# A two-block transformer forward pass: memory's key and value weights used whole, the rope tables issued in two parts, output weights by rows

## The chip, the cores and the metric

The kernel runs on one core of one Trainium2 chip. The metric is the time of the whole program on the device, in microseconds.

## The reference

A first block and then a second block of two layers work on 256 tokens of 1024 channels in fp32. Only the first block (and one line of the second) is touched. Cut to what matters it is:

```python
xn = rmsnorm(h, norm_mix_g)
q, k, v, u, y = split(xn @ w_in)             # 512 columns each
q, k = rope(q, positions), rope(k, positions)
attn = dilated_mixture_attention(q, k, v)    # 8 heads of 64
rec = bidirectional_rglru(conv(u), ...) * gelu(y)
h = h + concat([attn, rec]) @ w_out          # 1024 x 1024
hn, mn = rmsnorm(h, norm_cross_g), rmsnorm(mem, norm_mem_g)
q, k, v = hn @ w_cq, mn @ w_ck, mn @ w_cv    # 1024 x 512 each, 4 heads of 128
h = h + softmax(q k^T / sqrt(128)) v @ w_co  # 512 x 1024
hid = square(relu(rmsnorm(h, norm_mlp_g) @ w_mlp_in))
h = h + hid @ w_mlp_out
```

The second block has four mixers a layer (one of them, `mla`, is latent attention with norms of queries and keys) and a gated MLP.

## The kernel before

Activations lie channel by token, in 8 groups of 128 channels by 256 tokens. All large weights are streamed from HBM by SP in one array, `W`, in blocks of eight 128x128 tiles (512 KB, five buffers `w`). Each block is split in two f32r parts: ACT copies it to `whi` (L357) and DVE subtracts, `wlo` (L358), four buffers each. Activations are split the same way (`xh`, `xl`). A product of the precision wanted is then three f32r matmuls: `mm3` (L382 to L384: high by high, high by low part of the activation, low part of the weight by high). `lin` goes through a projection output chunk by output chunk, pairs of 128 columns sharing a PSUM bank; `lin_k` goes row by row of the weight, with all four chunks open in banks side by side; `lin_t` (L649 to L651) uses the activation as the stationary side and gives token by channel. Such results are used by consumers that are put off (`pend`, `flush`, `tick`) so that other work can go between.

Block 1 runs, in order, through w_in's part u (`lin_k`), q, k, v, y, then w_ck (memory's keys), w_out, w_cq, w_cv (memory's values), w_co, and the MLP. Beside these, generators put other work in between: the recurrence (`rglru`), the 8 heads of attention, memory's norm (`mem_prep`), the 4 heads of cross attention. `drive` and `interleave` step them at the chunks' ends, and a list scheduler writes each engine's queue with priorities (`high_priority`, `urgent`); the queues are fixed when the program is built, and each engine works through its own in order.

The first norm of the block needs a power, which runs on POOL (`rpow`, L401, `n1r`); its result is spread over partitions by two matmuls (L419, `n1p`), copied by ACT (L480, `n1b`), and every consumer of w_in multiplies by it. POOL also computes the angles of the rope tables from the positions (`rope_tables`, tiles `rt`, L845 and L850, with one cast L865), 50 small instructions of 128x64, then clears two large tiles (`gb`, L776). `derived` computes small parameters of the recurrence by a series on DVE (tiles `l`, L814 and L816). ACT takes the sine of the angles (L901, L902, `misc<-rt`), and eight matmuls (`rsp`, L911) spread the tables.

A head of attention has scores on PE (L1115, `sc`), scores plus bias and their maximum on DVE (L687, two instructions), the negated maximum (L693, `nm`), two exponentials on ACT (L699, `p`), the reciprocal of the sum on DVE (L702, `rd`), two scalings of `p` on ACT (L710, `times`), four transposes on PE (L717, `ptp`), a copy on ACT (L720, `pts`) and the values on PE (L727, `po`). Cross attention is the same with L1197 for scores and L1207 for values; its scores start at fixed points of w_cv. ACT and DVE then split the heads' output (`mxh`, `mxl`, or `ch`, `cl`), the moving side of w_out and w_co. In w_out the attention half of the rows comes first, and `rec` (the recurrence's output times the gate) is computed before w_out starts.

Of the kernel before, what the change touches and what calls it, by code (L numbers as in the profile page):

```python
# [15 lines left out]
OP = mybir.AluOpType  # L16
# [9 lines left out]
LAYERS = 2  # L26
BRANCHES = (1, 0, 2, 3)
NL, NX = 3, 4
# [5 lines left out]
X0, X1 = 1, 3  # L34
# [32 lines left out]
def plan():  # L67
# [4 lines left out]
    def f(key, idx, cols):  # L72
        p.append((key, idx, cols, "F"))

    def t(key, idx, cols):
        p.append((key, idx, cols, "T"))
# [11 lines left out]
    f("w_out", (0,), r(1024))  # L88
    tf("w_cq", (0,), r(512))
    t("w_cv", (0,), r(512))  # L90
    f("w_co", (0,), r(1024))
# [22 lines left out]
def stream_array(inp):  # L114
    tiles = []
    for key, idx, cols, kind in plan():
        w = np.asarray(inp[key])[idx][:, cols]
        k, n = w.shape
        w = w.reshape(k // 128, 128, n)
        if kind == "F":  # L120
# [154 lines left out]
class Kern:  # L275
    def __init__(self, ctx, tc, a, pcols, ccols, depth=5, ahead=2):
# [25 lines left out]
        for key, idx, cols, kind in plan():  # L302
            self.plan.append((key, idx, len(cols), kind))
        self.seg = 0
# [57 lines left out]
    def wtile(self, n=1):  # L362
# [7 lines left out]
        if o + n == size:  # L370
            self.blk_split.pop(self.pi)
            self.pi += 1
        return hi[:, o * 128:(o + n) * 128], lo[:, o * 128:(o + n) * 128]
# [22 lines left out]
    def rpow(self, name, src, n, mul, add):  # L396
# [4 lines left out]
        self.nc.gpsimd.tensor_tensor(r, v, self.mhalf[:, :n], op=OP.pow)  # L401
# [111 lines left out]
class Body(Kern):  # L513
# [42 lines left out]
    def lin(self, key, idx, M, act, consume, K=KD, fine=False, half=False, m0=0, side=False):  # L556


        for m in range(0, M, 2):
# [3 lines left out]
            for i, (c, k) in enumerate(self.order(key, idx, M, K, m, side)):  # L563
# [10 lines left out]
                if c == n - 1 or one or half:  # L574
# [47 lines left out]
    def lin_k(self, key, idx, M, act, consume, K=KD):  # L622

        self.segment(key, idx, M * 128, "T")
        ps = [self.ps("plk").rearrange("p (c t) -> p c t", c=2) for _ in range(M // 2)]
# [13 lines left out]
    def lin_t(self, key, idx, ncols, act, consume, K=KD, steps=2):  # L639
# [37 lines left out]
    def softmax(self, ps, scale, bias=None, normalize=True):  # L677
# [25 lines left out]
        if normalize:  # L703
            self.times(p, rd)
# [81 lines left out]
    def derived(self):  # L786
# [13 lines left out]
        nc.gpsimd.tensor_tensor(u, one, nab, op=OP.pow)  # L800

# [16 lines left out]
        nc.vector.tensor_tensor(lp, acc, z, op=OP.mult)  # L818
# [13 lines left out]
    def rope_tables(self):  # L832
# [45 lines left out]
        w = tt(turns(k2, P2), turns(k1, P1), OP.add)  # L878
        w = tt(w, rnd(w, 1.0), OP.subtract)
# [68 lines left out]
    def block1(self):  # L948
# [8 lines left out]
        self.derived()  # L957
        self.rope_tables()
# [3 lines left out]
        mh = [self.g4(f"mh{i}", F32R) for i in range(2)]  # L962
        ml = [self.g4(f"ml{i}", F32R) for i in range(2)]
        rm = {}

        def mem_prep():
            nm = Norm(self, eng=V)
            for j in range(4):
# [21 lines left out]
        self.setup_late()  # L990
# [151 lines left out]
        mact = lambda k: (mh[k // 4][:, k % 4], ml[k // 4][:, k % 4])  # L1142
# [4 lines left out]
        def c_cv(half, ps):  # L1147
# [15 lines left out]
        def residual(norm, g, scale=None, also=None):  # L1163
            def f(k, ps, n):
# [8 lines left out]
                if also:  # L1173
# [4 lines left out]
        run(self.lin("w_out", (0,), 8, lambda k: (mix_h[k // 4][:, k % 4], mix_l[k // 4][:, k % 4]),  # L1178
                     residual(n2, self.G("norm_cross_g")), fine=True))
# [657 lines left out]
```

## Time and profile before

| | us |
|---|---|
| runs | 1291.26, 1288.01, 1279.97 (median 1288.01) |
| profiled execution | 1285.87 |
| its span, first to last instruction | 1284.1 |
| PE busy in the span | 1253.4 |
| DVE, ACT, POOL busy | 917.8, 721.5, 85.3 |

Times of the trace count from the start of the span; 1.8 us of the execution lie around it. An idle time in front of an instruction is what its engine waited, and the name behind it is what came last. The granted clock (PEclk) is a share of TensorE's full 2.4 GHz: 1.00 is that level, 0.50 the 1.2 GHz one.

### The profile page before, as it was taken

The numbers are of one execution on the slowest core, as the hardware profiler recorded it, in microseconds if no ns is written. First come the engines' busy times: TensorE is split into PE (matmuls) and PEld (weight loads), VectorE is DVE, ScalarE is ACT, GpSimd is POOL, SyncE is SP. The second block draws the span as 40 slices with busy tenths as digits, with TensorE's granted clock in tenths as the row PEclk, the third lists the DMA queues.
The fourth block names the chain that finished last, engine by engine and source line by source line (L and its number), as shares of the span: only waits on it lengthen the run. The fifth ranks groups of instructions, "written<-read, shape, count | busy, mean of one in ns | idle before, by whom it ended". The sixth has DMA issues, their size and how long they took to land.

```text
span 1284.1 us, 21656 instructions
## 1 busy us (share of the span) xinstructions
PE 1253.4 (98%) x8514; PEld 1143.5 (89%) x8514; DVE 917.8 (71%) x1396; ACT 721.5 (56%) x1132; POOL 85.3 (7%) x105
## 2 busy tenths in 40 slices
PE   8998989999999999999999999999999999999998
PEld 7885978888899998899988888899988999888887
DVE  5996748875577985767777776669867677777754
ACT  5787556554456456644556554464565545655542
POOL 8010000000001201000000000012001000000000
PEclk9899999999999999999999999999998999999999
DMA  7742535555564551345555566544522355555662
GB/s 258 214 140 75 177 97 194 193 188 190 192 231 160 180 172 60 116 154 184 180 188 189 188 216 209 190 153 161 170 99 96 128 187 172 190 191 187 194 191 75
DMA packets 68742, 216.08 MB, mean 168 GB/s; under 512 B 10392, under 2 KB 16280, under 8 KB 68640
## 3 DMA queue, kind: packets, MB, share of 16 engines
q1 hardware_dynamic: 68592, 214.66, 50.9%
q8 instruction: 67, 1.10, 0.4%
q14 instruction: 35, 0.29, 0.1%
q0 software_dynamic: 48, 0.03, 0.0%
HBM read 208.37 MB, written 1.05 MB: 163 GB/s over the span
## 4 chain that ended last, share of the span: by engine, by line
PE 85%; ACT 2%; DVE 1%; DMA 1%; SPq 1%; issue 1%; DVEq 0%; ACTq 0%
PE pw L601 27%; PE pw L602 14%; PE pl L383 11%; PE pl L382 10%; PE pl L384 10%; PE ph L1428 2%; PE pl L649 1%; PE pl L650 1%; PE pl L651 1%; PE pq L1577 1%; SPq L1495 1%; DMA tabs<-in_C_dram 1%; PE pod L727 1%; ACT p L699 1%; PE ptp L717 1%; PE mst L426 1%
## 5 line engine op out<-in xcount | busy, mean ns | idle before, releaser
L357 ACT ACTIVATE whi<-w 128x1024 fp32r<-128x1024 f32 (+1 forms) x386 | 404.2, 1050 | 456.3 <-issue 166.8
L358 DVE TENSOR_TENSOR wlo<-w,whi 128x1024 fp32r<-128x1024 f32 (+1 forms) x386 | 467.2, 1212 | 244.6 <-ACT whi L357 244.0
L601 PE MATMUL pw<-xx,whi 128*128 128x512 f32 x960 | 334.0, 393 | 0.0
L602 PE MATMUL pw<-xx,wlo 128*128 128x256 f32 x960 | 268.2, 280 | 0.0
L382 PE MATMUL pl<-xx,whi 128*128 128x256 f32 x912 | 261.3, 287 | 3.6 <-ACT whi L357 3.6
L384 PE MATMUL pl<-xx,wlo 128*128 128x256 f32 x912 | 261.9, 288 | 1.8 <-DVE wlo L358 1.8
L383 PE MATMUL pl<-xx,whi 128*128 128x256 f32 x912 | 261.2, 287 | 0.0
L601 PEld LDWEIGHTS pw<-xx,whi 128*128 128x128 f32 x960 | 179.6, 187 | 39.9
L382 PEld LDWEIGHTS pl<-xx,whi 128*128 128x128 f32 x912 | 175.7, 193 | 8.2 <-ACT whi L357 4.0
L602 PEld LDWEIGHTS pw<-xx,wlo 128*128 128x128 f32 x960 | 181.1, 189 | 0.2
L384 PEld LDWEIGHTS pl<-xx,wlo 128*128 128x128 f32 x912 | 175.8, 193 | 3.2 <-DVE wlo L358 2.1
L383 PEld LDWEIGHTS pl<-xx,whi 128*128 128x128 f32 x912 | 175.9, 193 | 1.0 <-issue 0.8
L601 PE MATMUL pw<-fw,whi 128*128 128x512 f32 x352 | 123.4, 395 | 1.2 <-DVE fw L391 1.2
L602 PE MATMUL pw<-fw,wlo 128*128 128x256 f32 x352 | 98.9, 281 | 0.8 <-DVE wlo L358 0.8
L601 PE MATMUL pw<-hd,whi 128*128 128x512 f32 x256 | 88.8, 394 | 0.0
L601 PEld LDWEIGHTS pw<-fw,whi 128*128 128x128 f32 x352 | 66.0, 187 | 16.7 <-DVE fw L391 1.5
L602 PE MATMUL pw<-hd,wlo 128*128 128x256 f32 x256 | 70.9, 277 | 0.0
L602 PEld LDWEIGHTS pw<-fw,wlo 128*128 128x128 f32 x352 | 66.5, 189 | 1.4 <-DVE wlo L358 1.4
L601 PEld LDWEIGHTS pw<-hd,whi 128*128 128x128 f32 x256 | 48.0, 188 | 11.2
L602 PEld LDWEIGHTS pw<-hd,wlo 128*128 128x128 f32 x256 | 48.0, 188 | 0.0
L383 PE MATMUL pl<-ol,whi 128*128 128x256 f32 x128 | 37.1, 291 | 0.4 <-DVE ol L391 0.4
L382 PE MATMUL pl<-oh,whi 128*128 128x256 f32 x128 | 37.4, 295 | 0.0
(427 smaller groups left out, 1979.2 us busy)
## 6 DMA issues: line engine op xcount, KB each, us to landing
w<-in_W_dram SPq DMA_DIRECT2D x378, 512.0 KB, 3.5
w<-in_W_dram SPq DMA_DIRECT2D x8, 256.0 KB, 4.6
sw<-in_S_dram SPq DMA_DIRECT2D x4, 512.0 KB, 5.7
h<-in_xT_dram SPq DMA_DIRECT2D x8, 128.0 KB, 4.8
mem<-in_memT_dram SPq DMA_DIRECT2D x2, 512.0 KB, 7.7
sw<-qe SPq DMA_DIRECT2D x16, 64.0 KB, 4.6
dt<-in_C_dram SPq DMA_DIRECT2D x4, 256.0 KB, 8.1
dqs<-dhi SPq DMA_DIRECT2D x16, 64.0 KB, 3.6
```

The source lines that it names most:

```text
L357: self.nc.scalar.activation(hi, w, AF.Copy)
L358: self.nc.vector.tensor_tensor(lo, w, hi.bitcast(F32), op=OP.subtract)
L382: mm(out, wh, xh, start=first, stop=False, skip_group_check=shared)
L383: mm(out, wh, xl, start=False, stop=False, skip_group_check=shared)
L384: mm(out, wl, xh, start=False, stop=last, skip_group_check=shared)
L426: self.nc.tensor.matmul(ps[:, h], s[:, h * 128:h * 128 + 128], e, start=(i == 0), stop=(i == len(squares) - 1))
L601: mm(po[c], wh, x, start=k == 0, stop=False, skip_group_check=True)
L602: mm(po[c][:, 0], wl, x[:, 0], start=False, stop=k == K - 1, skip_group_check=True)
L649: mm(o, xh[:, s], wh, start=(k == 0), stop=False)
L650: mm(o, xh[:, s], wl, start=False, stop=False)
L651: mm(o, xl[:, s], wh, start=False, stop=(k == K - 1))
L1428: nc.tensor.matmul(ps[:, k], hk[:, 2 * hp + k // 2, s], qz[:, 2 * hp + k // 2, s], start=True, stop=True)
```

## The change

`WHOLE`: the blocks of w_ck and w_cv are not split, and neither is memory. Their products are one plain fp32 matmul in the place of three f32r ones (`wl is None`). The streamed block itself is then the operand, so its buffer is held until PE has used it, and the prefetch is limited by that (`kept`).

The rope tables and `derived` become generators in two parts. The first part of each is issued before the first norm's power, the second after it (`issue_after`), with the clearing of `gb`. The series of `derived` is written with seven fused instructions.

The first 512 columns of w_out and w_co go by `lin_k` (four chunks side by side), the other 512 by `lin`. The rows of w_out come in `OUT_ORDER`, the recurrence's half first, and `rec` runs before attention has to be done. The scaling of `p` moves from ACT to DVE (all softmaxes but those of one mixer, which calls `times` itself). Cross attention is driven as an urgent generator over w_cq and w_cv, with its value step later (`X1`). Norms 1 and 2 are spread one step earlier. In `mla` the power of the keys and queries `mrn` is computed before the other, `mqs`.

```diff
+WHOLE = ("w_ck", "w_cv")
+OUT_ORDER = (4, 5, 6, 7, 0, 1, 2, 3)
-X0, X1 = 1, 3
+X0, X1 = 1, 5
...
-    f("w_out", (0,), r(1024))
+    t("w_out", (0,), r(512), OUT_ORDER)
+    f("w_out", (0,), 512 + r(512), OUT_ORDER)
...
-        while self.nd < min(b + self.depth, self.nblk):
+        while self.nd < min([b + self.depth, self.nblk] + [k + NW for k in self.kept[:1]]):
             self._dma()
...
+        if self.ns in self.whole:
+            self.kept.append(b)
+            self.blk_split[self.ns] = (w, None)
+            self.ns += 1
+            return
...
+        if wl is None:
+            mm(out, wh, xh, start=first, stop=last, skip_group_check=shared)
+            return
...
         if normalize:
-            self.times(p, rd)
+            for q in range(2):
+                nc.vector.tensor_scalar(p[:, q], p[:, q], rd[:, q:q + 1], None, op0=OP.mult)
...
-        nc.vector.memset(acc, 1.0 / 17.0)
-        for k in (15, 13, 11, 9, 7, 5, 3, 1):
+        nc.vector.tensor_scalar(acc, z2, 1.0 / 17.0, None, op0=OP.mult)
+        for k in (15, 13, 11, 9, 7, 5, 3):
             nx = self.small("l9", 8)
-            nc.vector.tensor_tensor(nx, acc, z2, op=OP.mult)
-            acc = self.small("l10", 8)
-            nc.vector.tensor_scalar(acc, nx, 1.0 / k, None, op0=OP.add)
+            nc.vector.scalar_tensor_tensor(nx, acc, 1.0 / k, z2, op0=OP.add, op1=OP.mult)
+            acc = nx
...
         w = tt(turns(k2, P2), turns(k1, P1), OP.add)
+        yield
         w = tt(w, rnd(w, 1.0), OP.subtract)
...
-        self.derived()
-        self.rope_tables()
+        small = self.derived()
+        next(small)
+        tables = self.rope_tables()
+        next(tables)
...
-        self.setup_late()
+        self.tick()
+        self.tick()
+        with self.tc.issue_after(self.last_pow.ins):
+            run(tables)
+            self.setup_late()
+        run(small)
...
-        mact = lambda k: (mh[k // 4][:, k % 4], ml[k // 4][:, k % 4])
+        mact = lambda k: (self.mem[k // 4][:, k % 4], None)
...
-                    self.lin("w_ck", (0,), 4, mact, c_ck, half=True), ("need", rg), ("need", at)])
+                    self.lin("w_ck", (0,), 4, mact, c_ck, half=True), ("need", rg), ("need", rec()), ("need", at)])
         self.flush()
-        run(rec())
...
-        run(self.lin("w_out", (0,), 8, lambda k: (mix_h[k // 4][:, k % 4], mix_l[k // 4][:, k % 4]),
-                     residual(n2, self.G("norm_cross_g")), fine=True))
+        run(self.lin_k("w_out", (0,), 4, xmix, res, bank=self.psl))
+        run(self.lin("w_out", (0,), 4, xmix, res, fine=True, m0=4))
...
-        interleave(self.lin_t("w_cv", (0,), 512, mact, c_cv, steps=4), [cross()])
+        at = urgent(self.tc, cross(), HA)
+        self.drive([("begin", at), self.lin("w_cq", (0,), 4, xact, c_cq, half=True, side=True),
+                    self.lin_t("w_cv", (0,), 512, mact, c_cv, steps=4), ("need", at)])
...
+            rn = self.rpow("mrn", st2[:, 8:16], 8, 1.0 / 96, EPS)
             qs = self.small("mqs", 8)
             nc.gpsimd.tensor_tensor(qs, v, self.mhalf[:, :8], op=OP.pow)
-            rn = self.rpow("mrn", st2[:, 8:16], 8, 1.0 / 96, EPS)
```

How the queues move shows at three places. In POOL's queue at the first norm's power (`n1r`; `rt` are the angles), before:

```order
L850 TENSOR_TENSOR rt_243<-rt_243,rt_242 128x64
L845 TENSOR_SCALAR rt_243<-rt_243 128x64 x4
L850 TENSOR_TENSOR rt_243<-rt_243 128x64 x2
L845 TENSOR_SCALAR rt_243<-rt_243 128x64 x2
L776 MEMSET gb_462 128x1024
L776 MEMSET gb_463 128x1024
L401 TENSOR_TENSOR n1r<-v,misc 128x2
L401 TENSOR_TENSOR mr<-v,misc 128x2
```

The same place after:

```order
L874 TENSOR_SCALAR rt_191<-rt_191 128x64
L879 TENSOR_TENSOR rt_191<-rt_190,rt_191 128x64
L874 TENSOR_SCALAR rt_191<-rt_191 128x64
L879 TENSOR_TENSOR rt_191<-rt_191 128x64 x4
L426 TENSOR_TENSOR n1r<-v,misc 128x2
L874 TENSOR_SCALAR rt_191<-rt_191 128x64
L874 TENSOR_SCALAR rt_191<-rt_190 128x64
L924 MEMSET misc 128x1
```

The power stood behind all 50 instructions of the tables and two clearings; now it stands behind 28 of them, and the rest follows it.

In ACT's queue at the sines (`misc<-rt`) and the copy of the spread norm (`n1b`), before:

```order
L357 ACTIVATE whi<-w 128x1024 x3
L902 ACT_TABLE_LOAD
L902 ACTIVATE misc<-rt_243 128x64
L901 ACTIVATE misc<-rt_244,misc 128x64
L357 ACTIVATE whi<-w 128x1024 x4
L480 ACTIVATE n1b<-n1p 128x256
L357 ACTIVATE whi<-w 128x1024
L1013 ACTIVATE uc<-ut,pt 128x256 x4
```

And after:

```order
L377 ACTIVATE whi<-w 128x1024 x3
L505 ACTIVATE n1b<-n1p 128x256
L377 ACTIVATE whi<-w 128x1024 x3
L932 ACT_TABLE_LOAD
L932 ACTIVATE misc<-rt_192 128x64
L377 ACTIVATE whi<-w 128x1024
L931 ACTIVATE misc<-rt_193,misc 128x64
L1049 ACTIVATE uc<-ut,pt 128x256 x4
```

The sines stood in front of four splits and the norm's copy; they now stand behind the copy and behind three of those splits. On PE the two `n1p` matmuls follow the norm's sums (`ss`) by 26 products in the place of some 78, and `rsp` follows `n1p` by some 78 in the place of 60.

In PE's queue where w_ck ends and attention's last heads remain, before (`ptp` transposes, `sc` scores, `po` values):

```order
L384 MATMUL pl<-mh_297,wlo 128x256
L717 MATMUL ptp<-ct,p 128x128
L1115 MATMUL sc<-kr,qr 128x256 x2
L717 MATMUL ptp<-ct,p 128x128 x3
L1115 MATMUL sc<-kr,qr 128x256 x2
L717 MATMUL ptp<-ct,p 128x128 x4
L727 MATMUL po<-pts,vv 64x256 x4
L717 MATMUL ptp<-ct,p 128x128
L1115 MATMUL sc<-kr,qr 128x256 x2
L717 MATMUL ptp<-ct,p 128x128 x3
L1115 MATMUL sc<-kr,qr 128x256 x2
L717 MATMUL ptp<-ct,p 128x128 x4
```

And after, from the last product of w_ck on:

```order
L405 MATMUL pl<-mem_500,w 128x256
L746 MATMUL ptp<-ct,p 128x128 x4
L756 MATMUL po<-pts,vv 64x256
L746 MATMUL ptp<-ct,p 128x128 x4
L756 MATMUL po<-pts,vv 64x256 x3
L1151 MATMUL sc<-kr,qr 128x256 x4
L756 MATMUL po<-pts,vv 64x256
L746 MATMUL ptp<-ct,p 128x128 x8
L756 MATMUL po<-pts,vv 64x256 x3
L746 MATMUL ptp<-ct,p 128x128 x4
L756 MATMUL po<-pts,vv 64x256 x5
L746 MATMUL ptp<-ct,p 128x128 x4
```

Four heads' scores stood behind w_ck; now two do, since two more heads' scores stand among w_ck's products. Behind these rows w_out begins in both; now 24 of its products (`plk`) stand in front of the last three value matmuls, where 13 stood among the last heads before.

## Rows read from the trace of the kernel before

**Rows 1.** The page: span, and busy time of the engines.
```profile
span 1284.1 us, 21656 instructions
...
PE 1253.4 (98%) x8514; PEld 1143.5 (89%) x8514; DVE 917.8 (71%) x1396; ACT 721.5 (56%) x1132; POOL 85.3 (7%) x105
```

**Rows 2.** Busy time by stretch, block 1.
```profile
core 0: us, PE busy (x) PEld busy (x) DVE busy (x) ACT busy (x) POOL busy (x), PEclk, DMA share, GB/s
28.90:32.34 3.44, 0.00 (x1) 0.01 (x1) 1.61 (x2) 1.61 (x4) 3.11 (x8) 0.95 0.00 0
32.34:42.22 9.88, 7.41 (x31) 6.82 (x32) 8.08 (x20) 4.21 (x6) 1.87 (x2) 0.50 0.74 217
42.22:101.10 58.88, 58.67 (x406) 54.08 (x406) 57.84 (x93) 49.97 (x82) 3.88 (x1) 1.00 0.58 178
101.10:126.00 24.90, 18.57 (x98) 11.05 (x97) 16.35 (x48) 20.44 (x53) 0.00 (x0) 0.93 0.15 46
171.70:186.00 14.30, 10.84 (x63) 8.49 (x61) 5.16 (x14) 9.65 (x26) 0.00 (x0) 1.00 0.26 89
```

**Rows 3.** Waits, 0 to 50 us: us in total, times, longest.
```profile
PE pl L382 <- ACT whi L357: 3.6, 2, 3.4
```

**Rows 4.** Timeline of POOL, 7 to 36 us: start, us, instruction [idle before].
```profile
18.20 1.91 POOL L850 TENSOR_TENSOR rt<-rt 128x64 f32<-128x64 f32 x2
20.19 1.17 POOL L845 TENSOR_SCALAR rt<-rt 128x64 f32<-128x64 f32 x1
...
25.20 1.17 POOL L850 TENSOR_TENSOR rt<-rt 128x64 f32<-128x64 f32 x4
...
35.25 1.73 POOL L401 TENSOR_TENSOR n1r<-v,misc 128x2 f32<-128x2 f32 x1 [2.78 <-DVE misc L822]
```

**Rows 5.** Timeline of DVE, same stretch.
```profile
20.05 1.21 DVE L358 TENSOR_TENSOR wlo<-w,whi 128x1024 fp32r<-128x1024 f32 x1
...
30.73 0.23 DVE L891 TENSOR_TENSOR rt<-rt 128x64 f32<-128x64 f32 x1 [7.81 <-POOL rt L845]
```

**Rows 6.** Timeline of PE, 19.5 to 38 us.
```profile
19.90 0.50 PE L426 MATMUL ss<-ct,sq 128*128 128x1 f32 x4
...
37.04 0.69 PE L419 MATMUL n1p<-ct,n1r 128*128 128x128 f32 x2 [0.67 <-POOL n1r L401]
```

**Rows 7.** Timeline of PE, 60 to 68 us: fp32 and f32r products.
```profile
63.57 1.03 PE L1030 MATMUL pga<-uc,gb 128*128 128x256 f32 x4
64.44 1.03 PE L1031 MATMUL pgx<-uc,gb 128*128 128x256 f32 x4
...
67.16 0.39 PE L651 MATMUL pl<-whi,xx 128*128 128x512 f32 x1
...
67.84 0.39 PE L651 MATMUL pl<-whi,xx 128*128 128x512 f32 x1
```

**Rows 8.** Timeline of PE, 99.5 to 126 us: w_ck's end, attention's tail.
```profile
100.62 0.28 PE L384 MATMUL pl<-mh,wlo 128*128 128x256 f32 x1
...
100.98 0.28 PE L384 MATMUL pl<-mh,wlo 128*128 128x256 f32 x1
...
125.22 0.39 PE L383 MATMUL pl<-mxl,whi 128*128 128x256 f32 x1 [0.34 <-DVE mxl L391]
```

**Rows 9.** Instructions by line and shape, ACT, 76 to 124 us: busy, mean ns | idle.
```profile
L710 ACT ACTIVATE p<-p,rd 128x256 f32<-128x256 f32 x16 | 7.2, 499 | 1.5 <-DVE rd L702 1.5
```

**Rows 10.** The same view of DVE, whole span.
```profile
L1553 DVE TENSOR_SCALAR cqa<-cqa,pt 128x256 f32<-128x256 f32 x6 | 1.7, 347 | 0.0
```

**Rows 11.** Timeline of DVE, 99 to 118 us: heads 3 and 7.
```profile
104.74 0.40 DVE L687 CUSTOM_DVE_ANT_0 sb<-sc,lnc 128x256 f32<-128x256 f32 x1
...
115.30 0.42 DVE L687 CUSTOM_DVE_ANT_0 sb<-sc,lnc 128x256 f32<-128x256 f32 x1
```

**Rows 12.** Timeline of PE, 171 to 187 us: cross attention.
```profile
174.36 0.33 PE L717 MATMUL ptp<-ct,p 128*128 128x128 f32 x1 [1.35 <-ACT p L710]
```

**Rows 13.** Timeline of PE, layer 0's mla, 508 to 519 us.
```profile
516.45 0.60 PE L419 MATMUL rnb<-ct,rep 128*128 128x128 f32 x3 [1.00 <-DVE rep L416]
```

More of the change, by code (lines that the diff above doesn't have):

```diff
@@ L70, in plan, with f, t @@
     r = np.arange
[L72 to L76, printed above, removed]
+    def f(key, idx, cols, order=()):
+        p.append((key, idx, cols, "F", order))
+    def t(key, idx, cols, order=()):
+        p.append((key, idx, cols, "T", order))
     def tf(key, idx, cols):
@@ L115, in stream_array @@
     tiles = []
-    for key, idx, cols, kind in plan():
+    for key, idx, cols, kind, order in plan():
         w = np.asarray(inp[key])[idx][:, cols]
@@ L119, in stream_array @@
         w = w.reshape(k // 128, 128, n)
+        if order:
+            w = w[list(order)]
         if kind == "F":
@@ L301, in __init__ @@
         self.plan = []
-        for key, idx, cols, kind in plan():
+        for key, idx, cols, kind, _ in plan():
             self.plan.append((key, idx, len(cols), kind))
+        self.whole, self.kept, t = set(), [], 0
+        for key, _, n, _ in self.plan:
+            n = n // 128 * {"w_co": 4}.get(key, KD)
+            if key in WHOLE:
+                self.whole.update(i for i, (o, _) in enumerate(self.parts) if t <= o < t + n)
+            if key == "w_co":
+                break
+            t += n
         self.seg = 0
@@ L371, in wtile @@
             self.blk_split.pop(self.pi)
+            if self.pi in self.whole:
+                self.kept.pop(0)
             self.pi += 1
-        return hi[:, o * 128:(o + n) * 128], lo[:, o * 128:(o + n) * 128]
+        return hi[:, o * 128:(o + n) * 128], None if lo is None else lo[:, o * 128:(o + n) * 128]
     def segment(self, key, idx, ncols, kind):
@@ L573, in lin @@
                 self.tick()
-                if c == n - 1 or one or half:
+                if c == n - 1 or one or half or len(self.pend) > 1:
                     self.flush()
@@ L620, in joined, with lin_k @@
         return t
-    def lin_k(self, key, idx, M, act, consume, K=KD):
+    def lin_k(self, key, idx, M, act, consume, K=KD, bank=None):
         self.segment(key, idx, M * 128, "T")
-        ps = [self.ps("plk").rearrange("p (c t) -> p c t", c=2) for _ in range(M // 2)]
+        ps = [(bank or self.ps)("plk").rearrange("p (c t) -> p c t", c=2) for _ in range(M // 2)]
         for k in range(K):
@@ L648, in lin_t @@
                 s = slice(h * 128, h * 128 + 128)
+                if wl is None:
+                    mm(o, xh[:, s], wh, start=(k == 0), stop=(k == K - 1))
+                    continue
                 mm(o, xh[:, s], wh, start=(k == 0), stop=False)
@@ L979, in mem_prep @@
             rm["r"] = self.rpow("mr", nm.sums(), 2, 1.0 / D, EPS)
+            yield
+            yield
             yield
@@ L1185, in c_cq @@
             V.tensor_tensor(cq[:, k:k + n], ps, self.bT(r2["b"], n), op=OP.mult)
-        run(self.lin("w_cq", (0,), 4, xact, c_cq, side=True))
         ch, cl = self.g4("ch", F32R), self.g4("cl", F32R)
         def cross():
+            yield
+            yield
             live = {}
@@ L1211, in cross @@
                 yield
[L1213 removed]
+        at = urgent(self.tc, cross(), HA)
+        self.drive([("begin", at), self.lin("w_cq", (0,), 4, xact, c_cq, half=True, side=True),
+                    self.lin_t("w_cv", (0,), 512, mact, c_cv, steps=4), ("need", at)])
         n3 = Norm(self)
[L1215 removed]
+        res = residual(n3, self.G("norm_mlp_g"))
+        run(self.lin_k("w_co", (0,), 4, self.act(ch, cl), res, K=4, bank=self.psl))
+        run(self.lin("w_co", (0,), 4, self.act(ch, cl), res, K=4, fine=True, m0=4))
         self.flush()
```

16 lines of the change are left out of this document (8 added, 8 removed).

## The prediction

> **What bounds the kernel now.** I read the page's head first: PE is busy 1253.4 of 1284.1 us [rows 1], so an edit pays only where PE stands idle or runs at half clock, or where PE itself gets more or less to do. Then the busy time by stretch, since the change lies in the first 200 us: the reader is to compare PE's column with the length of each stretch, and to look at PEclk. Three stretches lose time [rows 2]. A, the first norm: 3.44 us with nothing on PE, then 9.88 us of which 7.41 are busy at a clock of 0.50, so 3.44 + 2.47 idle and 7.41/2 = 3.7 that full clock would have saved, 9.6 us. B, attention's tail between w_ck and w_out: 24.90 less 18.57 is 6.3 idle, and 24.9 x 0.07 = 1.7 for the mean clock of 0.93, 8.0 us. C, cross attention's tail: 14.30 less 10.84, 3.5 us. Between A and B PE is idle 0.2 us of 58.88, but DVE is busy for 57.84 of it; DVE follows close behind PE there.
>
> The waits and the timelines tell what A is. PE waits 3.4 us in one piece for a split [rows 3], and DVE stood idle 7.81 us for POOL's last angle [rows 5]: ACT's sines stand in the queue before the splits. POOL starts the power only at 35.25 and takes 1.73 [rows 4], and PE reaches `n1p` just then, having been slowed [rows 6].
>
> **The change part by part.** A. The power now stands behind 28 of POOL's instructions. The first 20 end by 20.1 as before (18.20 + 1.91), and the next was stretched to 1.17 [rows 4] while DVE subtracted for 1.21 from 20.05 [rows 5]; with DVE idle four took 1.17 together, 0.29 each [rows 4]. For the 8 that are left I take 0.5 each, since DVE is busy part of the time: 24.1. With 1.73 the power is done at 25.9. PE, after the sums at 19.90 [rows 6] and 26 products at 0.12 each (three in 0.36, [rows 8]), is at `n1p` at about 23.2. It waits some 2.8 us. Bounds: 8 at 0.29 give 22.4 and 24.1, a wait of 0.9; 8 at 1.17 give 29.5 and 31.2, a wait of 8. I choose near the low end because `derived`'s series and the tail of the splits leave DVE with little to do. After `n1p` PE has some 78 products, 9.4 us, until `rsp`, at 26 + 9.4 = 35.4. The second part of the tables is 22 instructions, a clearing of one number among them; at 0.29 to 0.6 each (the first 20 took 12.1 us beside a busy DVE, since POOL began at 8.0, 0.6 each) that is 6.4 to 13, so the angles come at 32 to 39, and the sines and the spread about 1 us later. I take 36.5, a wait of about 1, and 1 for a clock that falls after the wait at `n1p`. A then loses 2.8 + 1 + 1 = 4.8 instead of 9.6: -4.8. The clearing of `gb` (nothing reads it until the gates' products near 60 us) and the shorter series (16 small instructions on a DVE that is idle) cost and give nothing.
>
> Whole products. Two fp32 products of 128x256 are 0.87 apart in one line's four records [rows 7], 0.43 each; a triple of the other kind takes 0.36 [rows 8]. w_ck has 4 chunks by 8 rows: 32 x 0.07 = +2.2. w_cv has 16 products 512 wide: twice 0.43 against 0.68 for a triple [rows 7], 16 x 0.18 = +2.9. Together +5.1 on PE, which is the bound; I take +5.4, since the 512-wide one is scaled from another shape (bounds 0.8 and 0.9 for it: 4 to 6). DVE and ACT lose 8 splits each of w_ck and w_cv and four of memory. That shortens PE only where it waits for them. The four w_ck splits at 1.21 [rows 5] lie in the stretch where DVE is full; part of w_out's come forward into it. Whole blocks hold their buffers until PE is done with them; in 101 to 126 the DMA share is 0.15 [rows 2], so the stream has room, and I cost that at nothing; if that cover is gone PE waits for a block once, up to 4 us.
>
> B. The scaling goes from 2 x 0.50 on ACT [rows 9] to 2 x 0.35 on DVE, by the rows of a scaling of the same shape [rows 10]. The chain of a head has one crossing of engines less, but its instructions stay: heads 3 to 7 begin on DVE at 104.74 and 115.30 [rows 11], 2.6 us a head, and I expect the same pace, since DVE, which sets it with ACT, gets more per head. What changes is the start: w_ck is longer, two more heads' scores lie in it, and two heads instead of four have theirs behind it. The tail from w_ck's end to w_out's steady flow at 125.22 [rows 8] had four heads behind it and 6.3 idle, 1.6 for each; with two behind it I take 3.2. The 24 products of w_out that now stand ahead of the last values cover some of that, 24 x 0.12 = 2.9, but PE must also wait inside w_ck if the heads' pace is slower than w_ck's products (six heads by 2.6 are 15.6 against 32 x 0.43 = 13.8); I set the one against the other and add 0.8. With 1.6 for a clock that falls as before that is 5.6 instead of 8.0, -2.4. Bounds: all waits hidden, -6; the heads' chain late because DVE has more to do, +2.
>
> C. The wait of 1.35 for ACT's scaling [rows 12] goes, and `lin_k` puts some two dozen products that need only the first two heads in front of the last two heads' values, which covers about half of the others. But all scores stand later in w_cv than before. 3.5 becomes 1.7: -1.8 (0 to -3).
>
> mla. PE waits 1.00 us for a spread of `mrn` in layer 0 [rows 13]; one power fewer stands in front of it. A power takes 1.73 in [rows 4]. I take that wait, -1.0 (0 to -1.0); in layer 1 I found no such wait.
>
> The sum against the profiled execution: 1285.87 - 4.8 + 5.4 - 2.4 - 1.8 - 1.0 = 1281.3, of which 1.8 lie around the span as before (1285.87 - 1284.1, [rows 1]). The profiled execution is 2.1 below the median of the runs, 1288.01, so on the median the same sum would give 1283; I forecast **1281**. The waits that the change can take away are 9.6 + 8.0 + 3.5 + 1.0 = 22.1 at most, and 5.4 are paid for it.
>
> The rule that speaks against it: with DVE idle POOL's instructions took 0.29, and beside a subtraction of two tiles 1.17 [rows 4, 5]. The Trainium skill, "SBUF — State Buffer", section "SBUF: two separate sides", says why: the pair of ports that DVE and GpSimd share is an exclusive lock held for a whole instruction, against a DVE operation with two SBUF inputs too. By that rule every instruction of POOL that meets a split waits for all of it, and the trace agrees at that one place. Were it so at each of the 8, the power would be done at 31.2; this is the third rival below.
>
> **The rivals.**
> First, nearly all waits go: POOL is quick since DVE is idle (wait 0.9 and little after it, A 1.5), the heads are done inside w_ck (B 2), C 0.7, mla nothing. That is -8.1 - 6.0 - 2.8 - 1.0 + 5.4 = -12.5: 1273. For it: DVE's idle 7.8 us in A and the freed splits. Against it: DVE is full in the long stretch, and the heads' pace is their chain.
>
> Second, what A gains is lost again: DVE is 98% busy from 42 to 101 [rows 2], so it is the bound there as soon as PE starts earlier, and PE waits for it by as much. Then 1285.87 - 2.4 - 1.8 - 1.0 + 5.4 = 1286. Against it: w_ck's splits and memory's leave that stretch.
>
> Third, on the other side: POOL is held by DVE, 1.17 an instruction. The wait at `n1p` is 8 us and the angles come at 31.2 + 22 x 0.6 = 44.4 at best, while PE, on from 31.2, is at `rsp` at 40.6: 3.8 more, and after such a wait half clock as in A before, 3.7. A then loses 15.5, 5.9 more than before, and with no gain in B since everything starts late: 1285.87 + 5.9 - 1.8 - 1.0 + 5.4 = 1294. The change as a whole turns slower where A loses as much as before, with the power done about 4.8 us later than I think, near 31. For it: the one stretched row. Against it: the other rows around it at 0.3.
>
> Fourth, the edit does not do what it says: PE meets the same waits under other names, the whole products alone count: 1291.
>
> **How the numbers follow.** Forecast 0.47, first rival 0.22, second 0.16, third 0.08, fourth 0.07. One per cent, 12.9 us, is about what a measurement of this kernel can tell from no change (the three runs lie 11 us apart). Only the first rival reaches it, at its end, and a forecast with the low bounds in A and B: faster 0.22. Slower by that needs the third with a stall of the stream: 0.05. Within 1%: 0.73. The range: down to the first rival with 4 for unknown costs, 1269; up to the third's lower half, 1292; the likeliest one's own range is 1275 to 1287.
>
> **What would show it.** In the profile after: the stretch A with a wait of PE at `n1p` for POOL of about 3 us and the power starting near 24; fp32 products of w_ck 0.43 apart and of w_cv 0.86; one head every 2.6 us on DVE, idle of about 4 us between w_ck and w_out; 1.7 in cross attention; no wait for `rep` in layer 0. It would be wrong if the power starts after 28, if PE shows idle in the 40 to 100 us stretch, if the granted clock stays at 0.50 for more than 5 us, or if w_ck and w_cv wait for DMA.

## The result, and the profile after

The changed kernel takes 1270.42 us (median of 1274.38, 1270.73, 1270.11 and 1269.04) against 1285.37: 0.9882 of the kernel before, 95% interval 0.9863 to 0.9902. Its profiled execution is the slowest of the four, 1274.38 us with a span of 1272.6, 11.5 us below that of before.

The page's head, as [rows 1]:

```profile
span 1272.6 us, 21529 instructions
...
PE 1253.0 (98%) x8466; PEld 1139.0 (89%) x8466; DVE 914.4 (72%) x1415; ACT 695.0 (55%) x1080; POOL 86.3 (7%) x105
```

PE's busy time has hardly changed, so the gain is idle time. Busy time by stretch, as [rows 2] (the columns are the same): the first norm, the long middle, attention's tail in two pieces, cross attention's tail.

```profile
20.00:36.00 16.00, 14.37 (x119) 14.12 (x119) 11.71 (x33) 9.19 (x14) 13.20 (x29) 1.00 0.80 285
36.00:97.50 61.50, 61.50 (x371) 54.39 (x370) 57.74 (x101) 44.84 (x78) 3.83 (x1) 1.00 0.59 180
97.50:113.00 15.50, 11.54 (x60) 6.54 (x60) 12.21 (x44) 10.38 (x28) 0.00 (x0) 0.89 0.15 54
113.00:126.00 13.00, 13.00 (x106) 12.33 (x106) 5.91 (x8) 5.13 (x7) 0.00 (x0) 1.00 0.24 83
167.00:185.00 18.00, 16.98 (x126) 15.79 (x125) 10.17 (x25) 10.63 (x24) 0.00 (x0) 1.00 0.31 108
```

At the first norm PE is idle for 1.6 us at full clock, where it had lost 9.6. The middle has no idle time, though DVE is busy for as many microseconds as before (57.74 of 61.50, where it was 57.84 of 58.88 [rows 2]). Attention's tail is idle for 15.50 - 11.54 = 4.0, cross attention's for 1.0. The timeline of POOL at the first norm, as [rows 4]:

```profile
18.37 0.24 POOL L874 TENSOR_SCALAR rt<-rt 128x64 f32<-128x64 f32 x1
...
19.19 3.40 POOL L879 TENSOR_TENSOR rt<-rt 128x64 f32<-128x64 f32 x4
22.55 0.71 POOL L426 TENSOR_TENSOR n1r<-v,misc 128x2 f32<-128x2 f32 x1
```

and of DVE, as [rows 5]:

```profile
19.06 1.22 DVE L378 TENSOR_TENSOR wlo<-w,whi 128x1024 fp32r<-128x1024 f32 x1 [0.96 <-ACT whi L377]
...
20.40 1.21 DVE L378 TENSOR_TENSOR wlo<-w,whi 128x1024 fp32r<-128x1024 f32 x1
23.30 0.20 DVE L835 RECIPROCAL l<-l 128x8 f32<-128x8 f32 x1 [1.68 <-POOL n1r L426]
```

Four instructions of POOL, most of their time beside the two subtractions, took 3.40 us, 0.85 each; the power, with DVE idle, took 0.71 and was done at 23.26. The timeline of PE, as [rows 6], [rows 8] and [rows 12]:

```profile
18.94 0.50 PE L451 MATMUL ss<-ct,sq 128*128 128x1 f32 x4
...
20.34 0.38 PE L409 MATMUL pl<-xx,wlo 128*128 128x256 f32 x1 [0.55 <-DVE wlo L378]
...
23.32 0.43 PE L444 MATMUL n1p<-ct,n1r 128*128 128x128 f32 x2
...
34.27 2.00 PE L941 MATMUL rsp<-misc,sel 128*128 128x64 f32 x16 [1.29 <-ACT misc L931]
...
79.94 7.50 PE L405 MATMUL pl<-mem,w 128*128 128x256 f32 x34
87.28 0.60 PE L746 MATMUL ptp<-ct,p 128*128 128x128 f32 x4
...
103.09 0.65 PE L756 MATMUL po<-pts,vv 128*64 128x256 f32 x2 [1.14 <-ACT pts L749]
...
106.55 0.81 PE L746 MATMUL ptp<-ct,p 128*128 128x128 f32 x4 [0.78 <-DVE p L733]
...
109.15 0.76 PE L756 MATMUL po<-pts,vv 128*64 128x256 f32 x2 [1.80 <-ACT pts L749]
...
149.36 7.03 PE L675 MATMUL pl<-w,mem 128*128 128x512 f32 x16
156.22 1.89 PE L1236 MATMUL sc<-ck,cq 128*128 128x256 f32 x8
...
171.04 0.51 PE L407 MATMUL plk<-ch,whi 128*128 128x256 f32 x2 [0.93 <-ACT ch L414]
```

PE came to `n1p` at 23.32, 0.06 us after the power's end, and had nothing to wait for. A merged row ends with its last matmul, and that overlaps what follows (79.94 + 7.50 is 87.44, but the next row starts at 87.28), so the price of a product is taken from start to start. 34 records of w_ck, two to a product, go from 79.94 to 87.28: 0.43 a product. 16 records of w_cv go from 149.36 to 156.22: 0.86 a product.

For comparing kernels I use one table: idle time of PE, and the time that a clock below 1.00 cost, summed over stretches of 2 us of each profiled execution, and the start of `n3p`, the spread of the norm behind w_co, by which block 1's work up to there can be set beside another kernel's. Each row is one execution.

| kernel | first norm, to 60 us | 60 to 96 | attention's tail | cross | n3p at |
|---|---|---|---|---|---|
| before | 5.9 + 3.7 | 0.2 | 6.3 + 1.5 | 3.5 | 212.3 |
| changed | 1.6 + 0 | 0 | 4.0 + 1.5 | 1.0 | 202.2 |
| changed, again | 1.8 + 1.7 | 0 | 3.1 + 1.6 | 1.0 | 202.8 |
| tables joined | 5.5 + 2.0 | 0 | 2.2 + 1.4 | 1.0 | 206.0 |
| tables only | 1.6 + 1.7 | 5.4 + 3.8 | 4.5 + 5.9 | 3.5 | 216.1 |
| split again | 1.7 + 0 | 3.5 + 0 | 3.4 + 4.4 | 2.1 | 205.7 |
| w_out, w_co by chunks | 1.5 + 0 | 0 | 3.7 + 1.6 | 1.8 | 202.4 |
| scaling on ACT | 1.9 + 1.7 | 0 | 1.8 + 0 | 1.5 | 201.4 |
| powers swapped back | 1.6 + 0 | 0 | 3.7 + 1.5 | 1.0 | 201.5 |
| w_cv split | 1.9 + 1.7 | 0 | 4.0 + 1.6 | 2.1 | 202.7 |
| no extra yields | 1.8 + 1.7 | 0 | 3.4 + 1.5 | 1.0 | 203.4 |
| tables only, yields | 2.2 + 1.7 | 4.6 + 1.7 | 5.6 + 6.2 | 3.5 | 213.5 |
| natural rows | 1.7 + 0 | 0 | 3.1 + 0 | 1.0 | 200.5 |
| mixed scaling | 1.4 + 0 | 0 | 1.8 + 0 | 1.0 | 198.6 |

Idle time comes first, the clock's loss behind the plus sign. From 200 us on the clock alone loses between 3.4 us (split again) and 8.5 us (no extra yields) in these executions; the changed kernel lost 8.4 in one and 3.4 in the other. So times of kernels that differ by less than 3 us say little, and I go by the table. It has its own noise: the two executions of the changed kernel differ by 1.7 us of clock at the first norm, by 0.9 of idle time at attention's tail and by 0.6 at `n3p`.

### The profile page after: what moved, and what is told of

It is laid out like the page before. It is cut to its first block, busy times and chain, and to the rows that moved or that the text cites. A ratio compares the mean times of both kernels' runs of the same rounds, so it can differ in the third digit from the quotient of the medians.

```text
span 1272.6 us, 21529 instructions
## 1 busy us (share of the span) xinstructions
PE 1253.0 (98%) x8466; PEld 1139.0 (89%) x8466; DVE 914.4 (72%) x1415; ACT 695.0 (55%) x1080; POOL 86.3 (7%) x105
## 4 chain that ended last, share of the span: by engine, by line
PE 87%; DVE 4%; DMA 2%; POOL 2%; ACT 2%; issue 1%; SPq 1%; ACTq 0%; DVEq 0%; POOLq 0%
PE pw L626 28%; PE pw L627 14%; PE pl L407 10%; PE pl L408 10%; PE pl L409 10%; PE ph L1471 2%; PE pl L675 1%; POOL rt L874 1%; ACT p L727 1%; PE pq L1620 1%; PE pl L677 1%; PE pl L678 1%; PE pl L679 1%; SPq L1538 1%; DVE wlo L378 1%
## 5 line engine op out<-in xcount | busy, mean ns | idle before, releaser
L377 ACT ACTIVATE whi<-w 128x1024 fp32r<-128x1024 f32 (+1 forms) x378 | 395.9, 1050 | 459.6 <-issue 175.4
L378 DVE TENSOR_TENSOR wlo<-w,whi 128x1024 fp32r<-128x1024 f32 (+1 forms) x378 | 457.9, 1213 | 245.4 <-ACT whi L377 242.4
L409 PE MATMUL pl<-oh,wlo 128*128 128x256 f32 x128 | 37.3, 292 | 0.0
```

Of the source, the lines that this page charges most:

```text
L377: self.nc.scalar.activation(hi, w, AF.Copy)
L378: self.nc.vector.tensor_tensor(lo, w, hi.bitcast(F32), op=OP.subtract)
L409: mm(out, wl, xh, start=False, stop=last, skip_group_check=shared)
```

## The experiments

**Control.** The changed kernel, unedited.

> A control on the same chip as the next three: the changed kernel itself, 0.986 to 0.990 of the kernel before, and again no wait of PE at the first norm's spread.

0.9886, interval 0.987 to 0.9903, 1270.94 us; no wait at `n1p`. In this execution the clock fell once behind the wait at `rsp`, 1.7 us.

**Tables joined.**

```diff
-        small = self.derived()
-        next(small)
-        tables = self.rope_tables()
-        next(tables)
+        run(self.derived())
+        run(self.rope_tables())
...
-        with self.tc.issue_after(self.last_pow.ins):
-            run(tables)
-            self.setup_late()
-        run(small)
+        self.setup_late()
```

> The changed kernel with the rope tables and the series in one piece again, ahead of the first norm's power. Theory 1 (most of the gain is the first norm): 8 us of the gain are lost, 0.994 to 0.996 of the kernel before, with a PE wait for splits of over 3 us and half clock behind it. Rival (the gain comes from the splits that DVE and ACT no longer do; the norm's wait would then be short even with the tables ahead of it): at most 3 us lost, 0.988 to 0.990.

0.9916, 0.9904 to 0.9929: 0.003 or about 4 us lost against the control, between the two theories. PE and POOL at the first norm, from the timelines of this kernel:

```profile
33.91 0.69 PE L444 MATMUL n1p<-ct,n1r 128*128 128x128 f32 x2 [5.49 <-POOL n1r L426]
```

```profile
30.37 1.84 POOL L805 MEMSET gb<- 128x1024 f32 x2
32.18 1.68 POOL L426 TENSOR_TENSOR n1r<-v,misc 128x2 f32<-128x2 f32 x1
```

The wait is there, 5.5 us and 2.0 for the clock, but it is for the power itself and not for a split, and 2 us shorter in all than in the kernel before (7.5 against 9.6). The power starts at 32.18, right behind the clearings, where the kernel before had it at 35.25: there POOL stood idle for 2.78 us for DVE [rows 4], so POOL's queue alone did not hold it. Of the 4 us that the joined tables add over the control (7.5 against 3.5), attention's tail gives 1.1 back (3.6 against 4.7); `n3p` is 3.2 later.

**Tables only.** The kernel before with the two-part tables and series, the old series inside.

```diff
+        yield
         w = tt(w, rnd(w, 1.0), OP.subtract)
...
-        self.derived()
-        self.rope_tables()
+        small = self.derived()
+        next(small)
+        tables = self.rope_tables()
+        next(tables)
...
+        self.tick()
+        self.tick()
+        with self.tc.issue_after(self.last_pow.ins):
+            run(tables)
+            self.setup_late()
+        run(small)
```

> The kernel before with nothing but the tables and the series issued in two parts around the power. Theory 1: 8 to 9 us faster, 0.993 to 0.994, and the lead of about 9 us at the gates' products is still there where w_out ends. Rival (DVE is full from the norm to w_ck and w_ck's splits are still on it, so the lead is lost there): 0.998 to 1.000, with idle time of PE between 40 and 100 us.

1.0047, 1.0033 to 1.006: slower than before by 6 us. Theory 1 falls as a sum of parts. The first norm's gain is there (3.3 lost instead of 9.6), and 9.2 us are lost between 60 and 96, where the kernel before lost 0.2. The timelines of PE, POOL and DVE there:

```profile
74.33 1.14 PE L1124 MATMUL sc<-kr,qr 64*128 64x256 f32 x8 [1.43 <-DVE kr L1011]
79.48 0.48 PE L419 MATMUL mbp<-ct,mr 128*128 128x128 f32 x1 [4.03 <-POOL mr L401]
```

```profile
75.00 4.43 POOL L401 TENSOR_TENSOR mr<-v,misc 128x2 f32<-128x2 f32 x1 [40.10 <-DVE v L399]
```

```profile
74.70 0.15 DVE L399 TENSOR_SCALAR v<-ss 128x2 f32<-128x2 f32 x1
74.77 0.68 DVE L391 TENSOR_TENSOR ml<-mem,mh 128x512 fp32r<-128x512 f32 x1
75.37 3.49 DVE L358 TENSOR_TENSOR wlo<-w,whi 128x1024 fp32r<-128x1024 f32 x3
```

PE arrived sooner at work of DVE that had not become less. It waited for keys, then for memory's norm, whose sums PE had by 69.8 but DVE reached only at 74.70, and whose power took 4.43 beside DVE's subtractions. The busy time by stretch shows what followed:

```profile
72.90:82.00 9.10, 3.65 (x14) 2.22 (x15) 9.10 (x16) 8.99 (x10) 4.43 (x1) 0.71 0.46 145
82.00:100.00 18.00, 18.00 (x127) 17.48 (x127) 13.12 (x25) 13.04 (x20) 0.00 (x0) 0.86 0.36 125
100.00:128.00 28.00, 24.06 (x117) 15.34 (x115) 19.40 (x52) 22.65 (x57) 0.00 (x0) 0.76 0.18 62
```

DVE is busy for the whole 9.10 us and ACT for 8.99, PE for 3.65. Behind it the granted clock averages 0.86, and in the tail 0.76 where the kernel before had 0.93 [rows 2].

**Split again.** The changed kernel without the whole products.

```diff
-WHOLE = ("w_ck", "w_cv")
+WHOLE = ()
...
+                self.split(mh[j // 2][:, o:o + 2], ml[j // 2][:, o:o + 2], m[:, o:o + 2])
                 nm.add(sq)
...
-        mact = lambda k: (self.mem[k // 4][:, k % 4], None)
+        mact = lambda k: (mh[k // 4][:, k % 4], ml[k // 4][:, k % 4])
```

> The changed kernel with w_ck, w_cv and memory split again (three f32r products for each). Theory 2 (the whole products are a price of 5 us on PE that buys little): 2 to 5 us faster than the changed kernel, 0.984 to 0.987. Rival (they buy more than they cost, since DVE is full and two more heads go into w_ck): 2 to 5 us slower than the changed kernel, 0.990 to 0.992, with more idle time of PE between w_ck's start and w_out than the 4 us of the changed kernel.

0.9931, 0.9913 to 0.9948: 6 us slower than the control, of which `n3p` shows 2.9. Theory 2 falls, and the rival holds, at a little more than its 2 to 5 us. The profiled execution is the fastest of the six (1272.51, median 1277.34), so it shows only part of the 6. PE has 5.1 us less to do (below) and loses 15.1 us where the control lost 9.2, so 0.8 is left; `n3p` is 2.9 later, and 2.1 of that I have not traced to a wait. From the timeline of PE, and of DVE just before:

```profile
97.44 0.45 PE L746 MATMUL ptp<-ct,p 128*128 128x128 f32 x1 [4.08 <-DVE p L733]
```

```profile
91.60 1.22 DVE L378 TENSOR_TENSOR wlo<-w,whi 128x1024 fp32r<-128x1024 f32 x1
...
93.48 2.44 DVE L1104 TENSOR_TENSOR_SCAN tr<-e,ti 128x256 f32<-128x256 f32 x4
95.83 1.20 DVE L378 TENSOR_TENSOR wlo<-w,whi 128x1024 fp32r<-128x1024 f32 x1
96.94 0.61 DVE L733 TENSOR_SCALAR p<-p,rd 128x256 f32<-128x256 f32 x2
```

A head's `p` stands in DVE's queue behind the splits and the recurrence's scans. The busy time from 80 to 100 us, first in this kernel, then in the changed one:

```profile
80.00:100.00 20.00, 15.92 (x118) 14.65 (x118) 19.91 (x42) 10.50 (x20) 0.00 (x0) 0.90 0.59 192
```

```profile
80.00:100.00 20.00, 20.00 (x99) 15.71 (x98) 15.05 (x44) 9.88 (x25) 0.00 (x0) 1.00 0.60 208
```

Without the four splits of w_ck and of memory DVE is busy for 15.05 us of these 20 and PE never waits; with them DVE is busy for 19.91 and PE waits for 4.1. The splits come off ACT too, and no run takes them off one engine alone.

The whole products also carry the heads. In this kernel w_ck ends at 92.5, and four heads' scores stand behind it again, as in the kernel before (four records to a head, at 97.82, 100.65, 106.01 and 107.64):

```profile
97.82 2.07 PE L1154 MATMUL sc<-kr,qr 64*128 64x256 f32 x4
...
107.64 1.13 PE L1154 MATMUL sc<-kr,qr 64*128 64x256 f32 x4
```

Its tail loses 3.4 + 4.4 = 7.8 us, as much as the kernel before (6.3 + 1.5).

**w_cv alone split.** Memory is split besides, for w_cv alone.

```diff
-WHOLE = ("w_ck", "w_cv")
+WHOLE = ("w_ck",)
...
-                    self.lin_t("w_cv", (0,), 512, mact, c_cv, steps=4), ("need", at)])
+                    self.lin_t("w_cv", (0,), 512, lambda k: (mh[k // 4][:, k % 4], ml[k // 4][:, k % 4]), c_cv, steps=4), ("need", at)])
```

> The changed kernel with w_cv alone split again (memory is split for it, w_ck stays whole). If w_cv's whole product is a price without a return: 2 to 3 us faster than the changed kernel, cross attention's idle time no more than 2 us. Rival (the splits it spares give cross attention's softmax its room on DVE and ACT): not faster, idle time of 2.5 us or more at cross attention's tail.

0.9895, 0.9878 to 0.9913, `n3p` at 202.7: no difference from the control that can be told. w_cv's price of 2.9 is saved and `n3p` comes no sooner: 1.1 goes to idle time in cross attention (2.1 against 1.0), the rest I have not traced. The 6 us of the experiment before do not come back with w_cv, so the part that pays is w_ck.

**w_out and w_co by chunks.**

```diff
-    t("w_out", (0,), r(512), OUT_ORDER)
-    f("w_out", (0,), 512 + r(512), OUT_ORDER)
+    f("w_out", (0,), r(1024), OUT_ORDER)
...
-    t("w_co", (0,), r(512))
-    f("w_co", (0,), 512 + r(512))
+    f("w_co", (0,), r(1024))
...
-        run(self.lin_k("w_out", (0,), 4, xmix, res, bank=self.psl))
-        run(self.lin("w_out", (0,), 4, xmix, res, fine=True, m0=4))
+        run(self.lin("w_out", (0,), 8, xmix, res, fine=True))
...
-        run(self.lin_k("w_co", (0,), 4, self.act(ch, cl), res, K=4, bank=self.psl))
-        run(self.lin("w_co", (0,), 4, self.act(ch, cl), res, K=4, fine=True, m0=4))
+        run(self.lin("w_co", (0,), 8, self.act(ch, cl), res, K=4, fine=True))
```

> The changed kernel with w_out and w_co chunk by chunk again (eight chunks by lin), the order of the rows kept. If the chunks side by side cover the last heads: PE's idle time at attention's tail grows from 4.0 to 6 us or more and at cross attention's from 0.9 to 3, 4 us slower than the changed kernel. Rival (the order of the rows alone covers them): within 1 us of it.

0.9905, 0.9887 to 0.9924. The table shows no gain of the chunks side by side at attention's tail (3.7 against 3.1 and 4.0), 0.8 us at cross attention's, and `n3p` at 202.4. No gain up to there can be told. The median, 1274.37, is 3.4 us above the control's, with intervals that overlap; the profiled execution lost 3.4 us more to the clock behind 200 us, so the 4 us that were expected are neither shown nor excluded by the times.

**Natural rows.**

```diff
-OUT_ORDER = (4, 5, 6, 7, 0, 1, 2, 3)
+OUT_ORDER = (0, 1, 2, 3, 4, 5, 6, 7)
...
-                    self.lin("w_ck", (0,), 4, mact, c_ck, half=True), ("need", rg), ("need", rec()), ("need", at)])
+                    self.lin("w_ck", (0,), 4, mact, c_ck, half=True), ("need", rg), ("need", at)])
         self.flush()
+        run(rec())
```

> The changed kernel with w_out's rows in their natural order (attention's half first) and the recurrence's output made after attention, as before; the chunks still side by side. If the order of the rows covers attention's tail: idle time of PE between w_ck's end and w_out grows from 4 to 6 us or more, 2 to 4 us slower. Rival (the shorter tail comes from the heads that now lie in w_ck, whatever stands behind them): within 1 us.

0.9891, 0.987 to 0.9912, as the control; `n3p` at 200.5, 2 us sooner in this one execution, in which the clock's loss of 1.6 in the tail is absent. The order of the rows is not what shortened the tail. With the experiment before, the heads inside w_ck are left by elimination, and split again, where four heads stand behind w_ck and the tail is as long as before, agrees; but there DVE has its splits back as well, so the heads' place and DVE's room are not told apart.

**Scaling on ACT, and mixed.** First all of it on ACT:

```diff
-            for q in range(2):
-                nc.vector.tensor_scalar(p[:, q], p[:, q], rd[:, q:q + 1], None, op0=OP.mult)
+            self.times(p, rd)
```

then attention's eight heads alone (`act` is a new argument of `softmax`):

```diff
-                        live[s + i] = self.softmax(ps[i], 0.125, lnc)[0]
+                        live[s + i] = self.softmax(ps[i], 0.125, lnc, act=True)[0]
...
-        if normalize:
+        if act:
+            self.times(p, rd)
+        elif normalize:
```

> The changed kernel with the scaling of p on ACT again. If the scaling on DVE shortens the heads' chain: 2 to 3 us slower, idle time at attention's tail up from 4.0 to 6 us. Rival (it only moves 0.7 us a head from one engine of the chain to the other): within 1 us, the heads about as far apart on DVE.

> A combination: attention's eight heads scale p on ACT, cross attention and mla on DVE as in the changed kernel. If each is best where its engine has room: idle time at attention's tail falls from 4 to 2 us as with all scaling on ACT and cross attention and mla keep their short waits, 2 to 3 us faster than the changed kernel, 0.986. Rival: within 1 us of it, for the heads' tail is made up for by later waits.

0.9889, 0.9872 to 0.9905, and 0.9878, 0.9862 to 0.9894, 1269.64 us: neither can be told from the changed kernel by its time. In the table the expectation of the first is turned round: with ACT scaling, attention's tail is idle for 1.8 us in both kernels and the clock stays up, where the changed kernel was idle for 4.0 and 3.1 and lost 1.5 and 1.6 to the clock. So the move to DVE seems to cost 1 to 2 us of idle time there; it is not shown by the times, and the tables-joined kernel, which scales on DVE, is idle for only 2.2. From the mixed kernel, PE's last waits before w_out:

```profile
106.19 0.65 PE L758 MATMUL po<-pts,vv 128*64 128x256 f32 x2 [1.46 <-ACT pts L751]
107.20 1.13 PE L758 MATMUL po<-pts,vv 128*64 128x256 f32 x8 [0.36 <-ACT pts L751]
```

In cross attention PE is idle for 1.0 us with the scaling on DVE and for 1.5 with it on ACT. The mixed kernel's `n3p` at 198.6 is the earliest of all, 4 us ahead of the control, and its tail is as its expectation said; the 2 to 3 us of time did not show, since its median is 1.3 us lower, inside the noise.

**Powers swapped back.**

```diff
+            qs = self.small("mqs", 8)
+            nc.gpsimd.tensor_tensor(qs, v, self.mhalf[:, :8], op=OP.pow)
             rn = self.rpow("mrn", st2[:, 8:16], 8, 1.0 / 96, EPS)
-            qs = self.small("mqs", 8)
-            nc.gpsimd.tensor_tensor(qs, v, self.mhalf[:, :8], op=OP.pow)
```

> The changed kernel with the power mqs ahead of mrn again. If the order of the two powers is worth its wait: PE waits 1.0 and 0.4 us at layer 0's spread again, 1 to 1.4 us slower than the changed kernel, which is below what the times can tell; the lead over the kernel before between 500 and 930 us stays under 10 us instead of growing.

0.9913, 0.9899 to 0.9927. The wait at layer 0's spread does not come back: `rnb` starts at 508.77 with none. In its place PE waits at the end of mla in both layers, where the changed kernel has no wait; the timeline of PE in layer 0, and layer 1 reads the same at 994.64:

```profile
541.15 1.08 PE L756 MATMUL pom<-pts,vm 128*64 128x256 f32 x6 [0.39 <-ACT pts L749]
...
543.10 0.62 PE L407 MATMUL pl<-oh,whi 128*128 128x256 f32 x3 [0.87 <-ACT oh L414]
...
543.95 0.39 PE L408 MATMUL pl<-ol,whi 128*128 128x256 f32 x1 [0.24 <-DVE ol L416]
```

1.5 us a layer, about 3 in all, of some 3.5 us that its time shows. That these waits come from the order of the powers is not shown, since they also come and go where mla's own order is untouched. The scaling-on-ACT kernel, with the new order, has them; from its timeline of PE in layer 0:

```profile
539.64 0.62 PE L407 MATMUL pl<-oh,whi 128*128 128x256 f32 x3 [0.69 <-ACT oh L414]
...
540.84 0.39 PE L408 MATMUL pl<-ol,whi 128*128 128x256 f32 x1 [0.58 <-DVE ol L416]
```

The tables-only kernel, with the old order, waits there for 1.3 and 1.9 us in the two layers, and the kernel before, with the same mla, for 0.2 in each. The wait that I read, at layer 0's spread, comes back with the new order: 0.55 and 0.33 us in the natural-rows kernel, whose mla is that of the changed one. What sets either wait stays open.

**No extra yields, and tables only with them.** `mem_prep`, the generator of memory's norm, without its two extra yields in the changed kernel, so that the norm is spread two steps sooner; the tables-only kernel gets the same two lines with a plus.

```diff
             rm["r"] = self.rpow("mr", nm.sums(), 2, 1.0 / D, EPS)
             yield
-            yield
-            yield
```

> The changed kernel with memory's norm spread two steps earlier, as in the kernel before (mem_prep without its two extra yields). Theory 3 (behind the first norm DVE is full, POOL's power for memory's norm takes about 4 us beside it, and PE must not meet it early): PE waits 2 to 4 us for it between 65 and 80 us and the clock falls behind it, 3 to 6 us slower than the changed kernel. Rival (the wait of the tables-only run came from memory's splits on DVE alone): no such wait, within 1 us of the changed kernel.

> The tables-only kernel (the kernel before with the tables and the series in two parts) with the two extra yields in mem_prep besides. Theory 3: the wait of 4.0 us and the half clock behind it go, 5 to 8 us faster than tables-only, 0.998 to 1.000 of the kernel before, so still little gained: what is left of the lead is lost in front of w_ck's end, since w_ck's and memory's splits are still on a full DVE. Rival (the wait just moves behind the next product): no faster than 1.003.

The first: 0.9903, 0.9886 to 0.9921, no wait between 60 and 96, `n3p` 0.6 later. Its rival holds: once the splits are off DVE, memory's power (3.83 us here too) is early enough. The second: 1.0022, 1.0006 to 1.0038, 3 us faster than tables-only but no faster than before. The wait moved, as the rival said, if not as far as 1.003; from its timeline of PE:

```profile
74.15 2.07 PE L1126 MATMUL sc<-kr,qr 64*128 64x256 f32 x16 [1.54 <-DVE kr L1013]
...
79.32 0.39 PE L382 MATMUL pl<-xx,whi 128*128 128x256 f32 x1 [3.09 <-ACT vv L1106]
```

Moving one item in the queues helps little where both DVE and ACT are behind.

## Why the prediction was right or wrong

The direction and the range held; 1281 was 10 us too high, and the result lies near the range's low end, below the first rival's 1273. That rival came closer partly by luck: its terms for A (1.5) and C (0.7) nearly held, its B (2) did not, and 2.2 us of the gain before `n3p` belong to no term (below). In the profiled execution the gain is 11.5 where the sum had 4.6.

A. Forecast 4.8 us lost after, measured 1.6 (3.5 in the control). The term that was mis-sized is the power's end: 25.9 forecast, 23.26 measured. The tables have 48 instructions on POOL and not 50; 27 stand in front of the power and not 28, so 7 and not 8 were left after the first 20. These 7 took 22.55 - 18.37 = 4.2 us, 0.60 each where I had put 0.5, which made up for the one that was not there. But the first 20 ended 1.8 us sooner than in [rows 4] (18.3 against 20.1): they began at 7.45 for 8.00 and took 10.8 us for 12.1. And the power took 0.71 where I had put 1.73 from one row. That row stood beside a subtraction on DVE; from the timeline of DVE in the kernel before:

```profile
35.19 1.23 DVE L358 TENSOR_TENSOR wlo<-w,whi 128x1024 fp32r<-128x1024 f32 x1
```

The same trace has a power of this shape at 0.70, later in POOL's timeline:

```profile
387.21 0.70 POOL L401 TENSOR_TENSOR n5r<-v,misc 128x2 f32<-128x2 f32 x1 [0.76 <-DVE v L399]
```

I applied the rule of the shared port to the table's instructions but not to the power itself. The clock loss of 1 that I added came in one execution (1.7) and not in the other. The wait at `rsp` was 1.29 for a forecast of 1. PE's own arrival, 23.2, was right to 0.1 by luck: the sums began 1.0 us sooner (18.94 for 19.90 [rows 6]) and PE then waited 0.55 for a split, neither of which is in my sum. So the mechanism was right; the power's start was 1.5 us early against my 24.1, and its length was too long by a factor of 2.4.

Whole products. Forecast +5.4; measured 32 x (0.43 - 0.36) + 16 x (0.86 - 0.68) = 2.2 + 2.9 = 5.1, what the rows had given before I rounded up. The size is right and the reading was wrong: I took them for a price with little return ("that shortens PE only where it waits for them"). Splitting again makes the kernel slower, by 6 us in the medians and 2.9 at `n3p`: 5.9 us of waits and clock come back, a little more than the price, and the rest is not traced. The return is the part that the second rival named. DVE was 98% busy from 42 to 101 [rows 2], and the second rival (what A gains is lost again) is what tables-only shows, and more than lost, since PE's clock falls behind the waits. The changed kernel escapes it by what I wrote against that rival, that w_ck's and memory's splits leave the stretch. I had the two halves and did not couple them: the first norm's gain can only be kept together with the relief of DVE.

B. Forecast 8.0 to 5.6, measured 5.5 and 4.7. The step I named, more heads inside w_ck, is left as its cause: the tail is no longer than in the changed kernel when the chunks side by side or the order of the rows are taken back, and it is as long as before (7.8) when split again puts four heads behind w_ck. It was not tried by itself, and DVE's room changes with it. The scaling on DVE, which I set at no effect, seems to cost 1 to 2 us of idle time there.

C. Forecast 1.7, measured 1.0. Taking the chunks apart brings 0.8 of it back, the scaling 0.5, w_cv's splits 1.1.

mla. The wait of 1.0 [rows 13] is gone. It is gone with the old order of the powers too, and part of it is back with the new order in the natural-rows kernel: "one power fewer stands in front of it" was not the reason, and what was stays open.

Sum of block 1 by the table: 21.1 lost before, 8.1 after, less 5.1 for the products: 7.9. `n3p` is 10.1 earlier. Of the 2.2 between them 1.0 is a faster start (the sums at 18.94 for 19.90 [rows 6]); 1.2 us I have not traced. The median gained more than the profiled execution, 15 against 11.5: that execution is the slowest of its four and lost 5.0 us more to the clock behind 200 us than the control's did (8.4 against 3.4).

What stays open: what the order of the two powers is worth beside the clock in block 2, whether room on DVE or room on ACT is what the whole products buy, and a kernel that joins the mixed scaling, the natural order of the rows and one of the two whole products; it was not tried.

## What to carry to other kernels

An engine that is full but never waited for is a bound in hiding: DVE kept ahead of PE here only because PE was late. Before an early wait is removed, look at what stands behind it, and take work off that engine in the same step; here the early norm alone made the kernel 0.5% slower, the rest without it 0.8% faster, and both together 1.1 to 1.2%. PE time that frees such an engine (one fp32 product of 0.43 us for three f32r ones of 0.12) is one way to do it.

## What had not been expected

The same instruction on POOL, a power of 128x2, took 0.71 us with DVE idle, 1.73 [rows 4] and 1.68 (tables joined) where a subtraction had begun just before it, and between 3.35 (tables joined) and 4.96 (w_cv split) in the long middle, where DVE had no idle time beside them. The Trainium skill, "SBUF — State Buffer", section "SBUF: two separate sides", has the shared ports of DVE and GpSimd as an exclusive lock held for a whole instruction; the runs agree in part: the power that began 0.06 us into a subtraction of 1.23 us took 1.0 us longer than the one with DVE idle, most of what was left of that subtraction. A duration for POOL read from one row holds only for what DVE did at that moment.

The clock's loss can be as large as the waits before it: in tables-only 9.9 us of PE were idle between 60 us and w_out, and the lower clock cost another 9.7; in the tail alone 4.5 were idle and the clock cost 5.9.
